# Compressing keys and values side by side in one pass of the weights

## The chip, the cores and the metric

The kernel runs on one NeuronCore of a Trainium2 chip. The metric is the device time of one execution in microseconds (us). The core has a matrix engine (TensorE, "PE", with its weight loads shown as "PEld"), a vector engine (VectorE, "DVE"), a scalar engine (ScalarE, "ACT"), a general engine (GpSimd, "POOL") and SyncE ("SP"), whose queue issues most of the transfers from memory.

## The reference

One transformer block on 512 tokens of width 2048 in float32, batch 1. What matters here:

```python
proj = h @ w_in                                  # then split: conv parts, q, kc, vc, ksl, vsl, kw, vw, gates
# kc, vc: the raw keys and values to be compressed, 512 tokens x 2 heads x 128

def compress(kv, pe, w1, b1, w2):
    n_cmp = (S - 32) // 16 + 1                   # 31 blocks of 32 tokens, one every 16
    idx = np.arange(n_cmp)[:, None] * 16 + np.arange(32)[None, :]
    blocks = kv[:, idx] + pe[None, None, :, None, :]
    hid = gelu(einsum('bnlgd,ldh->bngh', blocks, w1) + b1)   # w1: 32 x 128 x 256
    return einsum('bngh,he->bnge', hid, w2)

k_cmp = compress(k_cmp_raw, pe_k, k_w1, k_b1, k_w2)
v_cmp = compress(v_cmp_raw, pe_v, v_w1, v_b1, v_w2)
k_cmp = apply_rope(rms_norm(k_cmp, k_norm[0]), ...)
# then: attention of q over k_cmp/v_cmp, over selected and over windowed keys; output projection; gated FFN
```

So keys and values go through the same form of product: for each of 32 positions `l`, a 128 x 62 matrix (2 heads x 31 blocks) is multiplied with a 128 x 256 weight slice, and the 32 products are summed.

## The kernel before

The kernel is one long program written out by Python loops and ordered at build time by a planner, which goes by what is written first and by what its own model holds to be ready; on each engine, and on SP's queue, the instructions then run in that fixed order. Large products are done in three passes of a split float32 (`mm3`, lines 98 to 100: `hi x lo`, `lo x hi`, `hi x hi`); `load_split` (lines 83 to 94) takes a 512 KB piece of weights into a tile `raw`, rounds it on ACT (line 92, `whi`) and forms the rest on DVE (line 93, `wlo`).

The stage of interest stands between the start of the kernel (the adaptive norm and the first columns of `w_in`) and the convolution with attention. Two generators are woven together (line 528): `token_blocks` (line 521) does the projections of windowed keys/values and of the second half of the queries, each as 8 steps of `token_block`. A step loads one 512 KB piece (line 91), splits it, and runs 24 matmuls of 128 x 128 by 128 x 512 into four `main` banks of PSUM. At the end of each block of 8 steps the banks are read: `take_kv` (lines 427 to 434) and `take_q` (lines 420 to 425) norm and rotate (`normed_rope`: squares on ACT line 405, the root on ACT line 407, products with the rope tables on DVE lines 412 to 417), turn on TensorE (lines 432, 424) and copy. The next user of `main` waits for these reads.

`before_attention` (line 512) is the other generator: for every step of `token_blocks` it gets 1.5 turns. It first takes the four parts of `ksv` (`take_kv(0, ...)`) and the four of `q0` (`take_q(0, ...)`), two 8 KB-per-partition tiles filled by the stage before, and then goes through `compress`. There, for keys and then for values (loop over `m`, line 457), DVE adds the position term to the raw keys or values (`blocks`, line 467); then in 8 turns of 4 positions each, 512 KB of weights come into a tile of the same ring of four `raw` buffers that `load_split` uses (line 473) and are used as they are, in plain float32, by four matmuls (line 476):

```python
for ll in range(4):
    nc.tensor.matmul(ph[:NP_, 0:256], blocks[:, l + ll, :, :].rearrange("p g n -> p (g n)"), rv[:, ll, :], ...)
```

`NP_` is 62. The profile shows each of these matmuls as two records, so 64 matmuls are 128 records. After each loop the bias is added (line 481), gelu is taken on ACT (line 482) and the result is turned (line 485, copies line 486). The end of `compress` (lines 487 to 509) forms the compressed keys `kcT` and values `v4`. `compress` has 17 turns.

After the weave, `convs` and `attention_steps` are woven: a step of `conv` (line 679 is its load, 680 and 681 its split) takes three `main` banks, the second of them first. In the convolution stage `ada_steps` also loads pieces of `ada_w` (line 179) and sums them on DVE (line 189).

A ring tile is free for the next load when its last reader has run: a `load_split` tile after DVE's line 93, a compress tile after its four matmuls.

## Time and profile before

| | us |
|---|---|
| median of three runs | 2312.16 (2307.25 to 2317.63) |
| the profiled execution, its time | 2311.1 |
| the profiled execution, its span of instructions | 2309.3 |
| TensorE busy in it | 2234.3 (97%) |
| VectorE busy in it | 1681.4 (73%) |
| ScalarE busy in it | 960.3 (42%) |

The busy time of TensorE is the union of its records, whose ends are modelled and overlap: what a matmul costs in a stream is read from the distance between starts, not from its duration. The time outside the span is 2311.1 - 2309.3 = 1.8 us.

### The profile page before, as it was taken

The page shows a single profiled execution, that of the slowest core. Times are in us where ns is not written, and L with a number is a line of the kernel's source. Part 1 is how long each engine was busy: PE and PEld are TensorE (multiplying, and loading weights), DVE is VectorE, ACT ScalarE, POOL GpSimd, SP SyncE. Part 2 cuts the span into 40 slices and gives each one's busy share as a digit, 9 for nine tenths or more (in the row PEclk, how much of TensorE's full clock was granted, in tenths as well). Part 3 has the DMA queues.
Part 4 walks back from the last instruction along what each step waited for, and adds up shares of the span by engine and source line. Part 5 has one row for each costly group of instructions (what it writes and reads, how often), then busy time and mean ns, then how long its engine had stood idle before and what let it go on. Part 6 is the DMA issues. An engine that isn't in the chain of part 4 may idle for free.

```text
span 2309.3 us, 30022 instructions
## 1 busy us (share of the span) xinstructions
PE 2234.3 (97%) x11225; PEld 1861.8 (81%) x11225; DVE 1681.4 (73%) x2561; ACT 960.3 (42%) x1601; POOL 132.7 (6%) x204
## 2 busy tenths in 40 slices
PE   5889999999999999899999999999999999999999
PEld 4667767778777778788888888888888788888887
DVE  6897738877856783888888888888888655534356
ACT  6544425455444222744444444444444432222221
POOL 2430000000000000000000000000000200000010
PEclk9999999999999999999999999999999999999999
DMA  8884356544533883264334443344442675533243
GB/s 292 262 277 148 98 189 184 165 126 147 147 94 128 301 291 128 87 183 123 119 120 124 123 123 120 119 123 124 123 124 78 216 245 187 182 106 128 92 155 114
DMA packets 374406, 358.60 MB, mean 155 GB/s; under 512 B 14856, under 2 KB 288620, under 8 KB 373236
## 3 DMA queue, kind: packets, MB, share of 16 engines
q1 hardware_dynamic: 365364, 325.22, 44.7%
q0 software_dynamic: 8896, 31.46, 3.9%
q8 instruction: 88, 1.44, 0.2%
q14 instruction: 58, 0.48, 0.1%
HBM read 336.70 MB, written 19.92 MB: 154 GB/s over the span
## 4 chain that ended last, share of the span: by engine, by line
PE 42%; issue 36%; DVE 10%; DMA 9%; ACT 2%; POOL 1%; SPq 0%; DVEq 0%; POOLq 0%; ACTq 0%
PE main L98 8%; PE main L99 8%; PE main L100 8%; DMA araw<-in_ada_w 7%; DVE acc L189 4%; PE aux L98 4%; PE aux L99 4%; PE aux L100 4%; PE aux L646 1%; DVE wlo L93 1%; PE main L834 1%; PE aux L834 1%; PE aux L618 1%; POOL gd L886 1%; DMA raw<-in_w_in 1%
## 5 line engine op out<-in xcount | busy, mean ns | idle before, releaser
L92 ACT CAST whi<-raw 128x1024 fp32r<-128x1024 f32 (+1 forms) x168 | 171.7, 1022 | 486.9 <-PE main L100 265.9
L93 DVE TENSOR_TENSOR wlo<-raw,whi 128x1024 fp32r<-128x1024 f32 (+1 forms) x168 | 200.4, 1193 | 223.2 <-ACT whi L92 221.7
L834 PE MATMUL main<-hC,whi 128*128 128x512 f32 x1408 | 356.2, 395 | 5.5 <-DVE hC L851 3.3
L827 DVE TENSOR_TENSOR wlo<-raw,whi 128x1024 fp32r<-128x1024 f32 x218 | 265.8, 1220 | 107.1 <-ACT whi L822 107.1
L189 DVE SCALAR_TENSOR_TENSOR acc<-araw,cT,acc 128x512 f32<-128x512 f32 (+1 forms) x392 | 270.8, 692 | 90.1 <-DMA araw<-in_ada_w 79.3
L822 ACT CAST whi<-raw 128x1024 fp32r<-128x1024 f32 x218 | 228.1, 1046 | 259.5 <-PE main L834 129.4
L834 PEld LDWEIGHTS main<-hC,whi 128*128 128x128 f32 x1408 | 254.4, 190 | 52.2 <-DVE hC L851 4.4
L834 PE MATMUL aux<-hC,whi 128*128 128x512 f32 x1072 | 269.5, 393 | 0.0
L834 PEld LDWEIGHTS aux<-hC,whi 128*128 128x128 f32 x1072 | 193.6, 190 | 34.8
L836 PEld LDWEIGHTS main<-hC,wlo 128*128 128x128 f32 x1408 | 192.9, 191 | 13.8
L836 PE MATMUL main<-hC,wlo 128*128 128x256 f32 x1408 | 197.0, 283 | 0.0
L98 PE MATMUL main<-alo,whi 128*128 128x512 f32 x448 | 180.9, 404 | 9.9 <-DVE alo L296 9.9
L100 PE MATMUL main<-ahi,whi 128*128 128x512 f32 x448 | 177.2, 396 | 0.0
L99 PE MATMUL main<-ahi,wlo 128*128 128x512 f32 x448 | 177.0, 395 | 0.0
L836 PEld LDWEIGHTS aux<-hC,wlo 128*128 128x128 f32 x1072 | 146.4, 190 | 10.5
L98 PE MATMUL main<-wlo,ahi 128*128 128x512 f32 x384 | 152.3, 397 | 0.5 <-DVE t L773 0.4
L100 PE MATMUL main<-whi,ahi 128*128 128x512 f32 x384 | 150.6, 392 | 0.0
L99 PE MATMUL main<-whi,alo 128*128 128x512 f32 x384 | 150.6, 392 | 0.0
L836 PE MATMUL aux<-hC,wlo 128*128 128x256 f32 x1072 | 149.8, 282 | 0.0
L822 ACT CAST whi<-t 128x1024 fp32r<-128x1024 f32 x84 | 88.2, 1050 | 136.4 <-PE aux L834 70.9
L98 PE MATMUL main<-wlo,ghi 128*128 128x512 f32 x352 | 138.2, 394 | 3.0 <-ACT ghi L1056 2.7
L98 PE MATMUL aux<-wlo,ghi 128*128 128x512 f32 x352 | 137.8, 391 | 0.0
(273 smaller groups left out, 3818.8 us busy)
## 6 DMA issues: line engine op xcount, KB each, us to landing
raw<-in_ffn_w SPq DMA_DIRECT2D x264, 512.0 KB
araw<-in_ada_w SPq DMA_DIRECT2D x136, 512.0 KB
araw<-in_ada_w SPq DMA_DIRECT2D x112, 256.0 KB
raw<-in_w_in SPq DMA_DIRECT2D x128, 192.0 KB
raw<-in_w_in SPq DMA_DIRECT2D x40, 512.0 KB
raw<-in_w_out SPq DMA_DIRECT2D x32, 512.0 KB
gd<-d POOLq DMA_DIRECT2D x44, 256.0 KB, 2.3
graw<-gd POOLq DMA_DIRECT2D x44, 256.0 KB, 4.1
```

The costliest lines, as they stand in the source:

```text
L92: nc.scalar.copy(hi[:, :m], raw[:, :m])
L93: nc.vector.tensor_sub(lo[:, :m], raw[:, :m], hi[:, :m].bitcast(F32))
L98: nc.tensor.matmul(ps, lhs[0], rhs[1], start=first, stop=False)
L99: nc.tensor.matmul(ps, lhs[1], rhs[0], start=False, stop=False)
L100: nc.tensor.matmul(ps, lhs[0], rhs[0], start=False, stop=last)
L189: nc.vector.scalar_tensor_tensor(acc, w, s, acc, op0=ALU.mult, op1=ALU.add)
L618: nc.tensor.matmul(one[b], queries(g, i, h), kT[b][g][:, :L], start=True, stop=True)
L646: nc.tensor.matmul(po[:, b * HD:(b + 1) * HD], s["pT"][b][:, kb * P:(kb + 1) * P], vv[b][:, kb, g * HD:(g + 1) * HD], start=kb == 0, stop= ...
L822: nc.scalar.copy(hi, t)
L827: nc.vector.tensor_sub(lo, t, hi.bitcast(F32))
L834: nc.tensor.matmul(ps, wt[0][:, ks[k]], hC[p][:, k, :], start=first and k == 0, stop=False, skip_group_check=True)
L836: nc.tensor.matmul(ps[:, HS:], wt[1][:, ks[k]], hC[p][:, k, 0:HS], start=False, stop=last and k == HK - 1, skip_group_check=True)
```

## The change

Both loops of `compress` become one. The tile `ph` now holds keys in partitions 0 to 61 and values in partitions 64 to 125. For each position one matmul for keys and one for values follow each other, into these two groups of columns of the array. `blocks` is made for 8 positions at a time, for keys and values (16 additions of half the former size, two buffers each), ahead of every second turn. The weights of the keys keep coming through the ring of `raw` tiles, and the load of the next turn is written ahead of the matmuls of this one. The weights of the values come into four places of 512 KB that are the halves of `ksv` and `q0`: the first four loads stand at the head of `compress`, each later one behind the matmuls that used its place. The bias is added for each half, and gelu, and the two turns of `hid`, are done once for both; `hid` is set to zero first by POOL. `compress` now has 9 turns.

```diff
--- before.py
+++ after.py
@@ -454,36 +454,66 @@
         nc.sync.dma_start(per[:, 0, :], a["cmp_pe_k"][0])
         nc.sync.dma_start(per[:, 1, :], a["cmp_pe_v"][0])
         hidT = cpool.tile([P, 2, 2, NP_], F32, name="hidT")
-        for m, (w1n, b1n) in enumerate((("cmp_k_w1", "cmp_k_b1"), ("cmp_v_w1", "cmp_v_b1"))):
+        peT = cpool.tile([P, 2, CMP_BLOCK], F32, name="peT")
+        for m in range(2):
             pt = aux()
             nc.tensor.transpose(pt[:, :CMP_BLOCK], per[:, m, :], ident[:CMP_BLOCK, :CMP_BLOCK])
-            peT = cpool.tile([P, CMP_BLOCK], F32, tag="peT", name="peT")
-            nc.vector.tensor_copy(peT, pt[:, :CMP_BLOCK])
-            blocks = cpool.tile([P, CMP_BLOCK, NKV, NC_], F32, tag="blocks", name="blocks")
+            nc.vector.tensor_copy(peT[:, m, :], pt[:, :CMP_BLOCK])
+
+        def blocks(m, l):
+
+            t = cpool.tile([P, 8, NKV, NC_], F32, tag=f"blocks{m}", name=f"blocks{m}", bufs=2)
+            h = l // 16 * 16
             for g in range(NKV):
-                for h in range(2):
-
-                    src = raw_kv[:, m, g, h * 16:h * 16 + NC_ * 16].rearrange("p (n r) -> p r n", r=16)
-                    nc.vector.tensor_add(blocks[:, h * 16:(h + 1) * 16, g, :], src,
-                                         peT[:, h * 16:(h + 1) * 16, None].to_broadcast([P, 16, NC_]))
-            ph = aux()
-            for l in range(0, CMP_BLOCK, 4):
-                raw = ring[0].tile([P, 1024], F32, tag="raw", name="raw")
-                rv = raw.rearrange("p (l h) -> p l h", l=4)
-                nc.sync.dma_start(rv, a[w1n][0, l:l + 4].rearrange("l d h -> d l h"))
-                yield
-                for ll in range(4):
-                    nc.tensor.matmul(ph[:NP_, 0:256], blocks[:, l + ll, :, :].rearrange("p g n -> p (g n)"), rv[:, ll, :],
-                                     start=l + ll == 0, stop=l + ll == CMP_BLOCK - 1)
-            b1 = cpool.tile([NP_, 256], F32, tag="b1", name="b1")
-            nc.sync.dma_start(b1, a[b1n].to_broadcast([NP_, 256]))
-            hid = cpool.tile([NP_, 256], F32, tag="hid", name="hid")
-            nc.vector.tensor_add(hid, ph[:NP_, 0:256], b1)
-            nc.scalar.activation(hid, hid, AF.Gelu_apprx_tanh)
-            for h in range(2):
-                pt = aux()
-                nc.tensor.transpose(pt[:, :NP_], hid[:, h * P:(h + 1) * P], ident[:NP_, :NP_])
-                nc.vector.tensor_copy(hidT[:, m, h, :], pt[:, :NP_])
+                src = raw_kv[:, m, g, h:h + NC_ * 16].rearrange("p (n r) -> p r n", r=16)[:, l - h:l - h + 8, :]
+                nc.vector.tensor_add(t[:, :, g, :], src, peT[:, m, l:l + 8, None].to_broadcast([P, 8, NC_]))
+            return t
+
+
+        ph = aux()
+        at_m = (slice(0, NP_), slice(64, 64 + NP_))
+
+        places = [t[:, i:i + 2, :].rearrange("p a (b h) -> p (a b) h", b=2) for t in (ksv, q0) for i in (0, 2)]
+
+        def load_k(l):
+            raw = ring[0].tile([P, 1024], F32, tag="raw", name="raw")
+            rv = raw.rearrange("p (l h) -> p l h", l=4)
+            nc.sync.dma_start(rv, a["cmp_k_w1"][0, l:l + 4].rearrange("l d h -> d l h"))
+            return rv
+
+        def load_v(l):
+            rv = places[l // 4 % 4]
+            nc.sync.dma_start(rv, a["cmp_v_w1"][0, l:l + 4].rearrange("l d h -> d l h"))
+            return rv
+
+        vs = [load_v(l) for l in range(0, 16, 4)]
+        ks = load_k(0)
+        for l in range(0, CMP_BLOCK, 4):
+            if l % 8 == 0:
+                bl = [blocks(m, l) for m in range(2)]
+            yield
+            rvs = (ks, vs[l // 4])
+            if l + 4 < CMP_BLOCK:
+                ks = load_k(l + 4)
+            for ll in range(4):
+                for m in range(2):
+                    nc.tensor.matmul(ph[at_m[m], 0:256], bl[m][:, l % 8 + ll, :, :].rearrange("p g n -> p (g n)"),
+                                     rvs[m][:, ll, :], start=l + ll == 0, stop=l + ll == CMP_BLOCK - 1,
+                                     skip_group_check=True)
+            if l + 16 < CMP_BLOCK:
+                vs.append(load_v(l + 16))
+        b1 = cpool.tile([P, 256], F32, name="b1")
+        hid = cpool.tile([P, 256], F32, name="hid")
+        nc.gpsimd.memset(hid, 0.0)
+        for m, b1n in enumerate(("cmp_k_b1", "cmp_v_b1")):
+            nc.sync.dma_start(b1[at_m[m], :], a[b1n].to_broadcast([NP_, 256]))
+            nc.vector.tensor_add(hid[at_m[m], :], ph[at_m[m], 0:256], b1[at_m[m], :])
+        nc.scalar.activation(hid, hid, AF.Gelu_apprx_tanh)
+        for h in range(2):
+            pt = aux()
+            nc.tensor.transpose(pt[:, :P], hid[:, h * P:(h + 1) * P], ident)
+            for m in range(2):
+                nc.vector.tensor_copy(hidT[:, m, h, :], pt[:, at_m[m]])
         cw2 = cpool.tile([P, 2, 2, HD], F32, name="cw2")
         nc.sync.dma_start(cw2[:, 0], a["cmp_k_w2"][0].rearrange("(h p) e -> p h e", p=P))
         nc.sync.dma_start(cw2[:, 1], a["cmp_v_w2"][0].rearrange("(h p) e -> p h e", p=P))
```

## Rows read from the trace of the kernel before

**Rows 1.** The page's first part: busy time of each engine, its share of the span, instructions.

```profile
PE 2234.3 (97%) x11225; PEld 1861.8 (81%) x11225; DVE 1681.4 (73%) x2561; ACT 960.3 (42%) x1601; POOL 132.7 (6%) x204
```

**Rows 2.** Busy time by stretch. Columns: stretch, its length, busy time of each engine (instructions), granted clock of TensorE as a share of full speed, busy share of the DMA engines, GB/s moved. The first two rows cover the two token blocks, the third the end of the second, the fourth the convolution and attention behind it.

```profile
core 0: us, PE busy (x) PEld busy (x) DVE busy (x) ACT busy (x) POOL busy (x), PEclk, DMA share, GB/s
...
219.00:270.00 51.00, 50.05 (x229) 39.18 (x229) 43.53 (x114) 25.59 (x77) 0.32 (x1) 1.00 0.30 92
270.00:341.00 71.00, 69.56 (x300) 48.49 (x299) 25.55 (x46) 14.46 (x27) 0.00 (x0) 1.00 0.56 180
341.00:350.00 9.00, 8.03 (x39) 4.72 (x38) 8.23 (x19) 7.25 (x30) 0.00 (x0) 1.00 0.71 199
350.00:600.00 250.00, 245.79 (x1256) 198.08 (x1255) 197.52 (x436) 125.22 (x283) 0.00 (x0) 1.00 0.53 157
```

**Rows 3.** Groups of instructions between 240 and 365 us, shapes kept apart. Columns: line, engine, operation, tiles, shapes, count | busy us, mean ns of one | idle time before them and what ended it.

```profile
L476 PE MATMUL aux<-raw,blocks 128*62 128x256 f32 x128 | 30.4, 384 | 1.3 <-ACT rq L407 0.7 <-DVE blocks L467 0.5
...
L476 PEld LDWEIGHTS aux<-raw,blocks 128*62 128x62 f32 x128 | 16.2, 135 | 13.8 <-issue 2.5 <-ACT rq L407 1.1 <-DVE blocks L467 0.9
...
L467 DVE TENSOR_TENSOR blocks<-raw_kv,peT 128x496 f32<-128x496 f32 x8 | 7.6, 1027 | 0.1
...
L415 DVE TENSOR_TENSOR rw<-q,Zq 128x256 f32<-128x256 f32 x8 | 3.0, 419 | 0.0
```

**Rows 4.** TensorE's instructions in order of time, around two bursts of line 476 inside the second token block. Columns: start, length, what; in brackets idle time before it and what ended it.

```profile
305.64 0.39 PE L100 MATMUL main<-whi,ahi 128*128 128x512 f32 x1
305.96 1.94 PE L476 MATMUL aux<-raw,blocks 128*62 128x256 f32 x8
307.83 0.50 PE L98 MATMUL main<-wlo,ahi 128*128 128x512 f32 x1
308.16 0.39 PE L99 MATMUL main<-whi,alo 128*128 128x512 f32 x1
308.39 0.39 PE L100 MATMUL main<-whi,ahi 128*128 128x512 f32 x1
...
324.36 3.67 PE L476 MATMUL aux<-raw,blocks 128*62 128x256 f32 x16
```

**Rows 5.** TensorE in order of time: the first of the 24 matmuls of steps 9, 10 and 11 of the token blocks.

```profile
274.12 0.48 PE L98 MATMUL main<-wlo,ahi 128*128 128x512 f32 x1
...
283.44 0.50 PE L98 MATMUL main<-wlo,ahi 128*128 128x512 f32 x1
...
292.75 0.50 PE L98 MATMUL main<-wlo,ahi 128*128 128x512 f32 x1
```

**Rows 6.** SP's queue in order of time (start, time spent on issuing and waiting, what): loads of the token steps are line 91, of the compression line 473.

```profile
247.04 8.65 SPq L473 DMA_DIRECT2D raw<-in_cmp_k_w  x2
266.82 0.37 SPq L91 DMA_DIRECT2D raw<-in_w_in  x1
...
273.81 7.83 SPq L473 DMA_DIRECT2D raw<-in_cmp_k_w  x2
283.55 0.37 SPq L91 DMA_DIRECT2D raw<-in_w_in  x1
```

**Rows 7.** The chain that ended last, in order of time (start, length, what): the load of token step 10 and its split.

```profile
273.08 5.84 DMA raw<-in_w_in
278.94 1.05 ACT whi L92
280.02 1.23 DVE wlo L93
```

**Rows 8.** VectorE in order of time: the last reads of `q0`, and the split of token step 9.

```profile
258.55 0.75 DVE L415 TENSOR_TENSOR rw<-q,Zq 128x256 f32<-128x256 f32 x2
...
271.83 1.23 DVE L93 TENSOR_TENSOR wlo<-raw,whi 128x1024 fp32r<-128x1024 f32 x1 [1.40 <-ACT whi L92]
```

**Rows 9.** ScalarE in order of time: the first half of the split of token step 11.

```profile
287.55 1.05 ACT L92 CAST whi<-raw 128x1024 fp32r<-128x1024 f32 x1 [7.55 <-DMA raw<-in_w_in]
```

**Rows 10.** TensorE in order of time at the end of the second token block: the last matmul of its step 16, and all that runs until the convolution (line 98 with `alo`) has begun.

```profile
340.85 0.39 PE L100 MATMUL main<-whi,ahi 128*128 128x512 f32 x1
341.16 3.67 PE L476 MATMUL aux<-raw,blocks 128*62 128x256 f32 x16
345.14 0.66 PE L424 MATMUL aux<-const,ru 128*128 128x128 f32 x4 [0.31 <-DVE ru L417]
345.72 1.94 PE L476 MATMUL aux<-raw,blocks 128*62 128x256 f32 x8
347.59 0.50 PE L98 MATMUL main<-alo,whi 128*128 128x512 f32 x1
```

**Rows 11.** VectorE in the same stretch: reads of the first and of the second `main` bank (lines 412 and 415), and what stands between.

```profile
339.81 0.75 DVE L189 SCALAR_TENSOR_TENSOR acc<-araw,cT,acc 128x512 f32<-128x512 f32 x1 [3.05 <-DMA araw<-in_ada_w]
340.48 0.68 DVE L412 TENSOR_TENSOR ru<-main,Cq 128x512 f32<-128x512 f32 x1
341.08 0.75 DVE L415 TENSOR_TENSOR rw<-main,Zq 128x256 f32<-128x256 f32 x2
...
345.08 0.66 DVE L412 TENSOR_TENSOR ru<-main,Cq 128x512 f32<-128x512 f32 x1
345.66 0.75 DVE L415 TENSOR_TENSOR rw<-main,Zq 128x256 f32<-128x256 f32 x2
```

**Rows 12.** Waits of TensorE between 235 and 385 us: who waited for whom, us in total, times, longest.

```profile
PE aux L424 <- DVE ru L417: 1.5, 3, 0.7
```

## The prediction

> **What bounds the kernel now.** I read the busy times first: TensorE is busy 97% of the span, the next engine 73% [rows 1]. A share is an average, so the second view is the stretches around the change [rows 2]. From 219 to 341 us, where the two token blocks and the compression run, TensorE is busy 119.6 of 122 us; VectorE is busy 25.55 of 71 us in the second part, ScalarE 14.46, and transfers take 0.56 of the DMA engines. [...] Time taken off TensorE in this stage should therefore move everything behind it, as long as nothing the removed matmuls covered comes to light. The third view says what the compression costs TensorE: 128 records of line 476, 62 columns of the array wide [rows 3]. In order of time [rows 4] a burst of 16 records lasts 3.67 us and one of 8 lasts 1.94, so one record costs (3.67 - 1.94) / 8 = 0.216 us; the 0.384 of the group is a modelled, overlapping length. All 128 cost 27.7 us.

> **Pairing.** A key matmul and a value matmul now go to different columns of the array. No row of before shows two matmuls that write different columns of the array side by side, so the price lies between two ends. At one end they don't overlap, and the 27.7 us stay. At the other, two records run at a time: 64 x 0.216 = 13.8 us, a gain of 13.8. Each matmul is two records, in the order key, key, value, value; if a record waits only for the one ahead in its own columns, the second key record runs beside the first value record, the second value record beside the next key record, and only the first and last of a burst of 16 stand alone: 9 places instead of 16. Eight such bursts are 8 x 9 x 0.216 = 15.6 us, a gain of 12.1. I take this one, since the columns 62 to 127 are idle in every record of line 476 and the two products share neither weights, data nor output partitions.

> [...]

> **Edges of bursts.** Where line 476 begins and ends, the starts are 0.32 and 0.33 us apart, against 0.23 between two matmuls of line 99 and 100 [rows 4]: 0.19 us a burst. Sixteen groups of 8 records become eight of 16, some of both merged with a neighbour: at most 8 x 0.19 = 1.5, I take 1.0. TensorE's wait of 0.5 us for the additions of the values [rows 3] goes too, as these now come in quarters. Gross: 12.1 + 1.0 + 0.5 = 13.6 us. The two turns of `hid` that are saved are worth at most 0.3 (half of the 0.66 us of a burst of four turns [rows 10]); I take nothing.

> **Work beside TensorE.** Eight additions of 128 x 496 at 1.027 us become sixteen of 128 x 248. The nearest size, 128 x 256, takes 0.419 [rows 3]: 6.7 us in all against 8.2, and at the very worst 16 x 1.027 = 16.4. VectorE idles 45 of 71 us there, which hides either; without that cover the worst case would cost 8.2. One gelu less, one bias addition as before for each half, and a clearing of `hid` on POOL, which is busy 0.00 in that stretch [rows 2] and depends on nothing: taken at nothing, hidden by TensorE's 69.56 us.

> **Transfers.** Sixteen loads of 512 KB stay sixteen. The first four value loads wait for the last readers of `ksv` and `q0`, of which the last ends at 258.55 + 0.75 = 259.3 [rows 8]. Queued behind them on SP is the load of token step 9, and through it ScalarE's rounding, VectorE's rest and TensorE; but that load was held until 266.82 anyway [rows 6], so the wait is hidden by 7.5 us. The later four value loads become ready at the end of a burst, just when the loads of token steps do (283.55 stands right behind a burst). So their price is that of a neighbour in the queue: the load of step 10, between two compress loads, took 5.84 us [rows 6, 7], that of step 11, alone, from 283.55 to 287.55, 4.0 [rows 6, 9]: 1.8 us for a neighbour. What TensorE can bear: step 9's split ends at 273.06 [rows 8] and its matmuls start at 274.12 [rows 5], 1.1 us; step 10: 281.25 [rows 7] to 283.44, 2.2; step 11: 287.55 + 1.05 + 1.23 = 289.83 [rows 7, 9] to 292.75, 2.9. One more neighbour each costs 0.7 at step 9 and nothing after; two cost (3.6 - 1.1) + (3.6 - 2.2) + (3.6 - 2.9) = 4.6, and with a fourth step like the third 5.3. I take 1.0, bounds 0 and 5.3. In the steps with compression a turn has 16 records, but if they pair it lasts 1.94 us as now, so these distances hold.

> **The end of the stage.** `compress` now has 9 turns, not 17; at 1.5 turns a step it is done at step 12 of 16. Before, three groups of it stood between the last matmul of step 16, which ends its stream at about 341.1, and the first of the convolution, 347.59: 3.67 + 1.94 us [rows 10]. They covered the reading of the second `main` bank, which the convolution needs first, and which VectorE ends at 345.66 + 0.75 = 346.4 [rows 11]. That cover is gone. If VectorE's order stays, TensorE stands idle 346.4 - 341.1 - 0.66 (a burst of turns) = 4.6 us; if it gets there without the 3.05 us that it waited for a piece of `ada_w` [rows 11], 1.6. The waits that this place already had, 1.5 us [rows 12], are inside that. Loss: 0.1 to 3.1, I take 1.5. What follows in `compress` (gelu, turns, compressed keys) moves from under the convolution to under steps 13 to 16, both bound by TensorE.

> **Sum.** 13.6 - 1.0 - 1.5 = 11.1 us off the profiled execution's 2311.1 (span 2309.3 and 1.8 around it): **2300.0**. That execution lies 1.1 below the median of the runs, so the two agree. With the ends of the terms: best 13.8 + 1.5 + 0.5 - 0.1 = 15.7, so 2295.4; worst 12.1 + 0.5 - 5.3 - 3.1 = 4.2, so 2306.9.

> **Rivals.**
> No overlap: the array runs one record after the other whatever the columns. Then 1.0 + 0.5 is gained and 1.5 lost at the end of the stage, and bursts of 3.67 us leave transfers more room: 2311, 2309 to 2313. For it: no row shows an overlap, and every record of line 476 here takes its full 0.216. Against: nothing is shared. This is also how the change would not do what it says. 0.20.

> SP's queue turns into the bound, the one that ends on the other side: a value load ahead of a token load waits for the burst directly before that token step. Then a whole load and split are bare: 4.0 to 5.84 + 1.05 + 1.23 [rows 7, 9], 7.2 us on the mean. Two such steps (14.4) take the gain; four, steps 10 to 13, give 2300 + 28.8 = 2329. For it: SP does stand still for 8.65 and 7.83 us at loads of line 473 [rows 6]. Against: the token loads wait for the same bursts already, and a planner that finds a token load ready first issues it first. 0.10.

> Weight loads bare: the pairs don't overlap and neither do loads of one half with matmuls of the other: 128 x 0.135 us [rows 3] = 17.3, so 2311 + 17 = 2328. [...] 0.06.

> **Chances and range.** The forecast holds 0.64. Half a per cent is 11.6 us, about what the measurement can tell from no change (the three runs lie 10.4 apart), and my gain of 11.1 stands on that edge: faster by more 0.40, within 0.24, as the term of the pairs may reach 13.8 and the start of the convolution may be free. No overlap: within 0.19, slower 0.01. SP's queue: slower 0.08, within 0.02. Bare loads: slower 0.05, within 0.01. Together faster 0.40, within 0.46, slower 0.14. The range goes from 2295 (0.05 below) to 2316, which takes in no overlap and leaves out 0.13; the likeliest case alone spans 2295 to 2307.

> **What would show it.** In the profile after, pairing is right if a burst of 16 records takes about 2.1 us rather than 3.67, with starts of key and value records nearly together; wrong if starts are 0.216 apart. The edge term shows as fewer bursts. The transfer term shows as idle time of TensorE before line 98 at steps 9 to 13, put down to `wlo`. The last term shows as idle time between the last matmul of step 16 and the convolution; more than 5 us there, or work of attention drawn forward to fill it, would put me wrong by some us either way, as would a planner that orders the convolution stage otherwise.

## The result, and the profile after

The changed kernel took 2293.88 us (median of four runs, 2292.26 to 2294.74) against 2313.31 for the kernel before (four runs, 2307.25 to 2317.63): a ratio of 0.9917, with an interval from 0.9893 to 0.9941. The forecast was 2300.0 with a range from 2295; the gain is about 19 us where 11.1 were worked out. The direction held, and so did the pairing; two losses that were charged against it did not come, and the time lies 1.1 us outside the range. (The same program, measured again in runs 5 and 8 below, gained 15 and 17 us.) The profiled execution took 2294.12 us, its span is 2292.4.

In the changed kernel line 476 (the matmuls of the compression) has become line 500, 467 (additions) 469, 473 (loads) 481 for keys and 486 for values, 482 (gelu) 511, 485 (turns of `hid`) 514, and 681 (split of the convolution's weights) 711. The first row is the page's busy time of each engine; [rows 1] answers to it.

```profile
PE 2220.5 (97%) x11223; PEld 1856.7 (81%) x11223; DVE 1684.2 (73%) x2569; ACT 958.6 (42%) x1598; POOL 132.0 (6%) x205
```

TensorE's busy time fell by 13.8 us, and its share stayed. By stretch (the columns of [rows 2]), the stage of the compression and what follows it:

```profile
219.00:270.00 51.00, 50.79 (x238) 39.53 (x238) 43.58 (x118) 25.39 (x75) 0.80 (x2) 1.00 0.47 144
270.00:341.00 71.00, 70.01 (x369) 52.14 (x368) 42.91 (x97) 23.89 (x64) 0.00 (x0) 1.00 0.61 188
...
350.00:600.00 250.00, 247.63 (x1257) 199.06 (x1256) 198.62 (x424) 126.68 (x291) 0.52 (x1) 1.00 0.53 152
```

Against [rows 2] TensorE is fuller in every stretch: it did not only lose work, it also lost idle time, 0.74, 0.45 and 1.84 us in these three. VectorE took over work of the convolution stage earlier (42.91 us busy where it was 25.55), and hid it.

TensorE in order of time, as in [rows 4]: first the first burst of line 500, then two turns that follow each other directly. `raw` is the weight of the keys, `ksv` or `q` that of the values.

```profile
263.24 0.61 PE L500 MATMUL aux<-raw,blocks 128*62 128x256 f32 x2
263.79 0.50 PE L100 MATMUL main<-whi,ahi 128*128 128x512 f32 x1
264.22 0.43 PE L500 MATMUL aux<-ksv,blocks 128*62 128x256 f32 x1
264.23 0.43 PE L500 MATMUL aux<-raw,blocks 128*62 128x256 f32 x1
264.49 0.38 PE L500 MATMUL aux<-ksv,blocks 128*62 128x256 f32 x1
264.49 0.38 PE L500 MATMUL aux<-raw,blocks 128*62 128x256 f32 x1
...
270.41 0.43 PE L500 MATMUL aux<-raw,blocks 128*62 128x256 f32 x1
270.42 0.43 PE L500 MATMUL aux<-ksv,blocks 128*62 128x256 f32 x1
270.68 0.38 PE L500 MATMUL aux<-raw,blocks 128*62 128x256 f32 x1
270.68 0.38 PE L500 MATMUL aux<-ksv,blocks 128*62 128x256 f32 x1
...
273.70 0.38 PE L500 MATMUL aux<-raw,blocks 128*62 128x256 f32 x1
273.70 0.38 PE L500 MATMUL aux<-q,blocks 128*62 128x256 f32 x1
274.01 0.66 PE L432 MATMUL aux<-const,ru 128*128 128x128 f32 x4
```

From 270.41 the 32 records of two turns start in pairs, the two of a pair at most 0.01 us apart, and the pairs follow each other about every 0.216 us: 274.01 - 270.41 = 3.60 us for 32 records, about the length of 16 before [rows 4]. So there are 8 places (of 0.216 us each) in a turn here, not the 9 of the forecast. Four matmuls, eight records, run without a partner: one key and one value matmul at the ends of the first turn, and one of each around 282.36 and 291.62, where the planner put the first key matmul of a turn ahead of a token step. In all the 128 records take 68 places.

The first burst says why. There the first key matmul (both records, 263.24) runs alone, a matmul of line 100 follows, and at 264.22 the first value record starts, when the additions of the values are done (its weight load, below, waits 0.25 us for line 469). A key record starts 0.01 us behind it. In program order the second record of that value matmul stands ahead of this key record, and yet the two start together: each half of the columns takes its own records in its own order here, and the key record of 264.23 does not wait for the value record of 264.49. Experiment 4 below shows how far that reaches.

The weight load of that first value record, and those of a pair (the view of TensorE's loads in order of time):

```profile
264.22 0.13 PEld L500 LDWEIGHTS aux<-ksv,blocks 128*62 128x62 f32 x1 [0.25 <-DVE blocks L469]
...
270.68 0.14 PEld L500 LDWEIGHTS aux<-raw,blocks 128*62 128x62 f32 x1
270.69 0.14 PEld L500 LDWEIGHTS aux<-ksv,blocks 128*62 128x62 f32 x1
```

Two loads of 0.14 us fall in a place of 0.216 and cost nothing to be seen.

TensorE's waits from 219 to 400 us (what it waited for, us in total, times, longest):

```profile
PE aux L732 <- ACT cc L730: 0.8, 1, 0.8
PE aux L514 <- ACT hid L511: 0.6, 1, 0.6
PE aux L667 <- DVE gsc L208: 0.4, 1, 0.4
PE aux L424 <- DVE ru L417: 0.4, 1, 0.4
PE aux L432 <- DVE ru L417: 0.2, 1, 0.2
```

In the same view of the kernel before, line 432 stood with

```profile
PE aux L432 <- DVE ru L417: 1.1, 2, 0.9
```

In the list of after no wait is for `wlo` and none for a weight. The 1.3 us of line 476 [rows 3] are gone, of the 1.5 us of line 424 [rows 12] 0.4 are left, and of the 1.1 of line 432 0.2; the wait for gelu (0.6) is new.

The end of the stage, TensorE in order of time and then VectorE's split of the convolution's first weights (line 711) and its reading of the `main` banks:

```profile
332.18 0.39 PE L100 MATMUL main<-whi,ahi 128*128 128x512 f32 x1
332.41 0.41 PE L98 MATMUL main<-alo,whi 128*128 128x512 f32 x1
```

```profile
322.99 0.95 DVE L711 TENSOR_TENSOR wlo<-raw,whi 128x768 fp32r<-128x768 f32 x1
...
331.48 0.73 DVE L415 TENSOR_TENSOR rw<-main,Zq 128x256 f32<-128x256 f32 x2
...
334.64 0.75 DVE L415 TENSOR_TENSOR rw<-main,Zq 128x256 f32<-128x256 f32 x2
```

The convolution's first matmul (332.41) stands 0.23 us behind the last one of step 16, the distance between two matmuls of lines 99 and 100 in [rows 4]. The bank that became free last before it is the one read until 331.48 + 0.73 = 332.2; the next was read until 334.64 + 0.75 = 335.4, long behind that start. The 1.6 to 4.6 us of idle time that the prediction saw here don't exist.

**Where the 20 us went.** I took the time from the start of each TensorE instruction to the next, less the idle time, grouped by line, and also the distance between the same matmul in both profiles. From the same matmul at about 219 us to the one at 590.36 before and 570.24 after:

| | before | after | difference |
|---|---|---|---|
| matmuls of the compression, start to next start | 29.6 | 15.7 | -13.9 |
| TensorE idle | 7.5 | 3.5 | -4.0 |
| the rest (turns, edges of bursts) | | | -2.4 |
| total | | | -20.3 |

From there to the end some 3 us are given back in this pair of profiles (the spans differ by 16.9), 2.4 of them between 770 and 860 us, where the granted clock is 0.93 and 0.91 in two stretches of after and 1.00 in those of before. No instruction of the change stands there; run 8 shows how much two executions of one kernel can differ in that way. The table is of one pair of executions too: in run 8's profile the idle time of this stretch is 4.9 us, not 3.5.

### The profile page after: what moved, and what is told of

The parts are those of the page before. It is cut to its first block, busy times and chain, and to the rows that moved or that the text cites. A ratio compares the mean times of both kernels' runs of the same rounds, so it can differ in the third digit from the quotient of the medians.

```text
span 2292.4 us, 30011 instructions
## 1 busy us (share of the span) xinstructions
PE 2220.5 (97%) x11223; PEld 1856.7 (81%) x11223; DVE 1684.2 (73%) x2569; ACT 958.6 (42%) x1598; POOL 132.0 (6%) x205
## 4 chain that ended last, share of the span: by engine, by line
PE 45%; issue 36%; DVE 9%; DMA 7%; ACT 2%; POOL 1%; SPq 0%; POOLq 0%; DVEq 0%; ACTq 0%
PE main L98 8%; PE main L100 8%; PE main L99 8%; DMA araw<-in_ada_w 5%; DVE acc L189 4%; PE aux L98 4%; PE aux L100 4%; PE aux L99 4%; PE aux L676 2%; PE aux L648 1%; DVE wlo L93 1%; DMA raw<-in_w_in 1%; POOL gd L916 1%; PE aux L864 1%; PE main L864 1%
## 5 line engine op out<-in xcount | busy, mean ns | idle before, releaser
L852 ACT CAST whi<-raw 128x1024 fp32r<-128x1024 f32 x218 | 228.2, 1047 | 259.3 <-PE main L864 129.1
L866 PEld LDWEIGHTS main<-hC,wlo 128*128 128x128 f32 x1408 | 192.9, 191 | 13.9
```

What stands on the lines that cost most here:

```text
L852: nc.scalar.copy(hi, t)
L866: nc.tensor.matmul(ps[:, HS:], wt[1][:, ks[k]], hC[p][:, k, 0:HS], start=False, stop=last and k == HK - 1, skip_group_check=True)
```

## The experiments

**What was to be told apart.** The first theory is the prediction's with the corrected count: the overlap of the column halves gives 64 x 0.216 = 13.8 us, and the rest is edges and waits. Its rivals: the gain, or what is above the 11.1, comes from the compression being over earlier; from the places, that is, from the weights no longer competing for ring tiles; or from the loads being asked for a step ahead. The first four kernels ran beside 23 runs of the kernel before (median 2315.56 us), the other four beside 17 (2314.82). None of them leaves out work. The expectations were written before the runs and say what each theory gives.

**1. No overlap: both products in the same columns.** Each product gets a bank of its own, and the bias is read accordingly; everything else is as in the changed kernel.

```diff
-        ph = aux()
+        ph = [aux(), aux()]
-                    nc.tensor.matmul(ph[at_m[m], 0:256], ...
+                    nc.tensor.matmul(ph[m][:NP_, 0:256], ...
...
```

> Keys and values in turn as in the changed kernel, with its loads, places and turns, but both products written to partitions 0 to 61, each in its own bank of PSUM, so that both use the same columns of the array. Theory A (the overlap of the two groups of columns is the gain): 128 records one after the other again, 64 x 0.216 = 13.8 us more than the changed kernel, about 2308 us (2305 to 2311), still some 5 below the kernel before. Theory B (most of the gain comes from loads, turns and an earlier end of the compression): within 4 us of the changed kernel, 2292 to 2298.

Measured: 2313.51 us (2309.98 to 2317.07), ratio 0.9985 (0.9977 to 0.9994), above both expected ranges and nearer to the first. TensorE in order of time, inside a burst of two turns:

```profile
273.02 0.59 PE L500 MATMUL aux<-ksv,blocks 128*62 128x256 f32 x2
273.45 0.59 PE L500 MATMUL aux<-raw,blocks 128*62 128x256 f32 x2
```

Two records per 0.43 us, one after the other: the matmuls of line 500 take 28.7 us. With the overlap undone, the change is worth 2.1 us by the medians (1.4 to 5.3 by the interval). Against run 3, on the same chip and with the same number of matmuls, the overlap is worth 2313.51 - 2295.94 = 17.6 us; against runs 5 and 8, which are the changed kernel on another chip, 13.7 and 15.8. 13.0 of it is line 500 itself (28.7 - 15.7). The rest is not put to single lines (TensorE waits 1.2 us for gelu here instead of 0.6), and it is no more than executions of one kernel differ by.

**2. Pairing alone: both weights through the ring, asked for ahead of their own turn.** The columns as in the change; no places (`load_v` takes a ring tile as `load_k` does), no lead.

```diff
-        vs = [load_v(l) for l in range(0, 16, 4)]
-        ks = load_k(0)
         for l in range(0, CMP_BLOCK, 4):
+            rvs = (load_k(l), load_v(l))
             yield
-            rvs = (ks, vs[l // 4])
...
```

> The pairing alone: both weights come through the ring of four raw tiles, loaded ahead of their own turn as in the kernel before; ksv and q0 are not used as places. Theory A: the overlap is what counts and loads are hidden, 2292 to 2297 us. Theory C (the places and the lead carry part of the gain, since a turn now needs two of four ring tiles and a token load waits for a burst): waits of TensorE for wlo of 2 to 6 us at each of the token steps 9 to 12, 2300 to 2315 us.

Measured: 2311.0 us (2306.41 to 2318.59), ratio 0.9979 (0.9969 to 0.9989), a gain of some 5 us, as the expectation's theory C has it, though most of the waits are for other weights than it names. TensorE's waits from 219 to 400 us, and one of them in order of time:

```profile
PE aux L497 <- DMA raw<-in_cmp_k_w: 7.5, 3, 3.5
...
PE main L98 <- DVE wlo L93: 1.3, 3, 0.6
```

```profile
306.12 0.99 PE L497 MATMUL aux<-raw,blocks 128*62 128x256 f32 x2 [3.51 <-DMA raw<-in_cmp_k_w]
```

The pairs overlap here too, but TensorE, which is now done with a turn in half the time, stands still until the next weights come: 7.5 us for key weights, and 1.3 for splits of the token blocks, of which the same view of before lists none. Behind the two longest of these waits, 3.14 and 3.51 us, the granted clock is 0.83 from 270 to 280 us and 0.57 from 306 to 310 (0.97 over all from 219 to 345, where the kernel before has 1.00), which adds to the loss. So most of the gain of the overlap reaches the end only because of where the weights go. (This run drops the lead along with the places; a lead without places was not run.)

**3. The compression stretched: two `yield` a turn, 17 turns as before.**

```diff
             yield
+            yield
```

> The changed kernel with two yields a turn, so that the compression has 17 turns again and ends with the second token block, as before. If my term for the end of the stage were right (bursts cover the reading of the main banks, and 1.5 us are lost without them), this is 1 to 3 us faster than the changed kernel: 2291 to 2293. If the early end is itself part of what the change gained beyond the overlap, it is 3 to 5 us slower: 2297 to 2299. If neither, the same within 2 us.

Measured: 2295.94 us (2294.34 to 2297.75), ratio 0.9914 (0.9901 to 0.9927): no slower than the changed kernel (0.9917, and 0.9925 and 0.9929 in runs 8 and 5), and not faster by more than its executions differ. That the compression's matmuls are over at 307 us instead of at the end of the stage (333.9 here) is not where the gain comes from. This takes away the rival of the early end. For the prediction's term of 1.5 us at the end of the stage these times alone would be too coarse; there the rows above decide.

**4. Four key matmuls, then four value matmuls.**

```diff
-            for ll in range(4):
-                for m in range(2):
+            for m in range(2):
+                for ll in range(4):
```

> The changed kernel with the four key matmuls of a turn first and its four value matmuls behind them, instead of in turn. If records start strictly in the order of the program, only the last key record and the first value record of a turn run together and nearly the whole 13.8 us come back: 2306 to 2309. If each group of columns takes its own records as soon as they are queued, whatever stands between, nothing is lost: 2292 to 2296.

Measured: 2300.78 us (2298.14 to 2307.91), ratio 0.9941 (0.9926 to 0.9956), between the two expected ranges. In the first turn the value records also wait for their additions, which end at about 266.1, so the burst to read is the second, of two turns. TensorE in order of time:

```profile
272.63 1.29 PE L500 MATMUL aux<-raw,blocks 128*62 128x256 f32 x5
273.55 0.43 PE L500 MATMUL aux<-ksv,blocks 128*62 128x256 f32 x1
273.76 0.38 PE L500 MATMUL aux<-raw,blocks 128*62 128x256 f32 x1
...
277.26 0.66 PE L432 MATMUL aux<-const,ru 128*128 128x128 f32 x4
```

Eight key records stand ahead of the first value record. That starts at 273.55, about when the fifth key record does: four key records go by alone at the start of the burst, four value records alone at its end, and what lies between is paired. The burst takes 277.26 - 272.63 = 4.63 us where the same 32 records take 3.60 in the changed kernel. Line 500 takes 20.0 us in all instead of 15.7; these 4.3 are most of the 4.8 between this run and run 3. So TensorE reached past waiting records of the other half here, but only past some four of them.

**5. Key weights not asked for a step ahead.** Places kept.

```diff
-        ks = load_k(0)
         for l in range(0, CMP_BLOCK, 4):
+            ks = load_k(l)
...
-            if l + 4 < CMP_BLOCK:
-                ks = load_k(l + 4)
```

> The changed kernel with the key weights loaded ahead of their own turn, as in the kernel before, instead of a step ahead; the places for the values stay. Theory C in the form that the places alone carry the gain of the loads: the same as the changed kernel, 2293 to 2298 us, and no wait of TensorE for raw tiles between 260 and 320 us. If the lead of the keys is needed: waits for key weights as in the run with both in the ring, 2300 to 2311.

Measured: 2299.77 us (2295.16 to 2302.93), ratio 0.9929 (0.9917 to 0.9942), between the two expected ranges and, beside run 8 (0.9925), the same as the changed kernel. But this run does not test the lead: the planner put all loads of SP's queue, and all instructions of every engine, into the order that they have in the changed kernel, over the whole trace. What was written differently came out the same, so this is one more measurement of the changed kernel (with a wait of 0.8 us for one split that the first profile does not have). What the lead is worth stays open.

**6. Two by two: two key matmuls, two value matmuls, and so on.**

```diff
-            for ll in range(4):
-                for m in range(2):
+            for ll, m in ((0, 0), (1, 0), (0, 1), (1, 1), (2, 0), (3, 0), (2, 1), (3, 1)):
```

> The changed kernel with two key matmuls, then two value matmuls, in turn. With four by four the first value record started beside the fifth key record, so TensorE reaches about four records past the one it runs. If that reach is the cause of the loss there, two by two (four records of each) loses next to nothing: within 2 us of the changed kernel, bursts of 16 records of 1.9 to 2.2 us. If every change from one group of columns to the other costs something, the loss lies between: 3 us.

Measured: 2295.66 us (2293.67 to 2298.09), ratio 0.9916 (0.9903 to 0.9928): nothing lost. The first key records, which run alone, and the start of the second burst:

```profile
263.84 1.05 PE L500 MATMUL aux<-raw,blocks 128*62 128x256 f32 x4
...
271.15 0.43 PE L500 MATMUL aux<-raw,blocks 128*62 128x256 f32 x1
271.17 0.43 PE L500 MATMUL aux<-ksv,blocks 128*62 128x256 f32 x1
```

The first four key records run alone because the values' additions are not done (the first value weight load, at 264.75, waits 0.32 us for line 469). In the second burst the first value record starts 0.02 us behind the first key record, although three more key records stand ahead of it. With four records between the halves TensorE still pairs, with eight it does not quite: the reach of about four records from run 4 holds.

**7. Places alone: the kernel before, with its value weights in the places of `ksv` and `q0`.** No pairing, no lead.

```diff
+            places = [t[:, i:i + 2, :].rearrange("p a (b h) -> p (a b) h", b=2) for t in (ksv, q0) for i in (0, 2)]
...
-                raw = ring[0].tile([P, 1024], F32, tag="raw", name="raw")
-                rv = raw.rearrange("p (l h) -> p l h", l=4)
+                if m:
+                    rv = places[l // 4 % 4]
+                else:
+                    raw = ring[0].tile([P, 1024], F32, tag="raw", name="raw")
+                    rv = raw.rearrange("p (l h) -> p l h", l=4)
```

> The kernel before, keys and then values in the same columns, with one part of the change alone: the value weights come to the places of ksv and q0 and no longer through the ring. Theory D (TensorE sets the time, the loads were hidden already): the same as before within 2 us, 2312 to 2317. Theory E (the ring was already holding the stage up, and what the change gained beyond the overlap comes from the places): 3 to 5 us faster, 2309 to 2312.

Measured: 2313.37 us (2308.8 to 2316.67), ratio 0.9987 (0.9978 to 0.9996): a gain of 1.5 us by the medians, 3 by the ratio (0.9 to 5.1 by the interval), inside theory D's range. Before the pairing nearly every load was hidden, so places had little to give. Pairing alone (run 2) gives 5 us and places alone 1.5 to 3, both together 15 to 19 (the result and runs 5 and 8): some 7 to 12 us are there only when both are done.

**8. The changed kernel once more, unaltered**, to see what two executions of it differ by.

> The changed kernel again, unchanged, beside the others: ratio to the kernel before 0.990 to 0.993. Its profile tells which of the differences in the stages behind the convolution (the granted clock at the turns of x2, and the waits of attention) are of the kernel and which of one execution.

Measured: 2297.7 us (2292.61 to 2303.3), ratio 0.9925 (0.991 to 0.994). Its profile (span 2300.3) is 8 us longer than the first profile of this kernel, with the same instructions in the same order. Of these 2.0 are there by 122 us, 2.8 between 307 and 332, 2.8 between 755 and 798. The last is two waits that are longer (for a piece of `ada_w` summed by VectorE, 3.6 us against 2.6, and 1.7, which the first profile lacks, for VectorE's scaling of the output projection's banks). The middle one can be followed to its start. First the chain that ended last and VectorE, ScalarE, TensorE in order of time; then the stretch from 316 to 320:

```profile
302.89 6.72 DMA raw<-in_w_in
```

```profile
310.80 1.23 DVE L93 TENSOR_TENSOR wlo<-raw,whi 128x1024 fp32r<-128x1024 f32 x1 [2.80 <-ACT whi L92]
311.94 0.85 DVE L510 TENSOR_TENSOR hid<-aux,b 62x256 f32<-62x256 f32 x2
...
312.87 1.28 ACT L511 ACT_TABLE_LOAD   x1 [2.10 <-DVE hid L510]
...
314.63 0.44 PE L514 MATMUL aux<-const,hid 128*128 128x128 f32 x2 [1.85 <-ACT hid L511]
...
316.50 0.63 PE L100 MATMUL main<-whi,ahi 128*128 128x512 f32 x1
316.93 0.63 PE L98 MATMUL main<-wlo,ahi 128*128 128x512 f32 x1
```

```profile
316.00:320.00 4.00, 4.00 (x12) 3.12 (x11) 2.16 (x8) 2.22 (x5) 0.00 (x0) 0.57 0.41 115
```

The load of a token step took 6.72 us here and 5.83 in the first profile, behind one of 6.43 us that took 5.86 in the first. TensorE bears that (its matmuls of that step come later), but on VectorE the bias additions of the compression (line 510, 311.94) stand behind the split (310.80), gelu and its table behind them, and the turns of `hid` on TensorE behind that. The wait of 0.6 us becomes 1.85. Then the granted clock is 0.57 from 316 to 320 us: matmuls start 0.43 us apart instead of 0.23, until 319.49. In the first profile the granted clock stayed at 1.00 in the same place after its wait of 0.63. Eight matmuls at 0.20 more are 1.6 us, more than the 1.2 by which the wait grew.

## Why the prediction was wrong in size and right in kind

**The bound** held: TensorE was and is the bound of the stage (from 219 to 341 us busy 119.6 of 122 us before and 120.8 after), and what came off it came off the end.

**Pairing, the largest term: 12.1 forecast, 13.0 measured.** The step "only the first and last of a burst of 16 stand alone: 9 places instead of 16" was wrong: 8 x 9 = 72 places were forecast, 68 were found, 60 of 0.216 us less than the 128 before. It supposed that the records start in program order; under the condition that it names, that a record waits only for the one ahead in its own columns, the count would have been 8. The rows show just that, two streams in which each half takes its own records; the four places above 64 are the matmuls without a partner, which the prediction did not have.

**Edges and waits of the values: 1.0 + 0.5 forecast.** The size was nearly right. Start to next start, line 476 took 29.6 us for 27.7 of work in 13 bursts, and line 500 15.7 for 14.7 (68 places) in 7: 0.9 less on the line itself. Another 0.09 (0.32 - 0.23) ahead of each of the six bursts that are gone, 0.5, is part of the 2.4 of the rest, of which 1.9 are not taken apart. The wait of 0.5 for the additions went, and with it the 0.7 for `rq` [rows 3], which I had not counted.

**Transfers: 1.0 of loss forecast, 0 in the first profile.** This is one of the two losses that did not come. The neighbours in the queue cost what was said: the load of one token step took 5.56 us, and the chain that ended last runs over it:

```profile
283.81 5.56 DMA raw<-in_w_in
289.40 1.06 ACT whi L92
290.48 1.24 DVE wlo L93
```

The split is done at 291.72 and the step's matmuls start at 292.14, behind a burst of two turns, so 0.4 us of the forecast's 2.9 were left, and at the step before 0.05 (split done at 282.83, matmuls at 282.88). The slack was used up almost exactly, and was enough; run 2 shows what happens when it isn't, run 5 has one wait of 0.8 us for a split, and run 8 shows that a late load can still come out by way of VectorE's order.

**The end of the stage: 1.5 of loss forecast, none found, and old waits gone.** This is the step that failed outright: "the second `main` bank, which the convolution needs first". The convolution started with the bank that was free, 0.23 us behind the matmul ahead of it, and 3 us before the second bank was read. [rows 11] could have told it: the first bank was read by 341.08 + 0.75 = 341.8, with the convolution at 347.59 [rows 10]. The bursts of line 476 stood ahead of the convolution in program order. What the first of them did cover is another wait, which the prediction did not look at, that for the split of the convolution's own first weights; VectorE in the kernel before:

```profile
343.52 0.95 DVE L681 TENSOR_TENSOR wlo<-raw,whi 128x768 fp32r<-128x768 f32 x1
```

That split ended at 344.5; after, the loads for it are issued from 305 us on instead of from 336, and it is done at 322.99 + 0.95 = 323.9, so nothing was left to cover. The waits that this stage already had, which I had left inside the loss, went down as well: lines 424 and 432 lose 1.2 and 0.9 us, and a wait of 1.0 us for a turn of attention at 586 us (line 664) has no counterpart after, which may be chance of the execution.

**Work beside TensorE** was hidden as said. The additions took longer than the 0.419 that I took from the nearest row: 16 in a median of 0.572 us, 9.2 in all instead of 6.7, still without effect, with one wait of 0.2 us of the loads on them.

**The sum.** Forecast 11.1; up to 590 us 20.3 were measured in the profiles. The difference of 9.2 is 0.9 (pairing) + 6.0 (idle time: 4.0 gained where 0.5 gained and 2.5 lost were forecast) + 2.3 (edges and the rest, 0.9 + 2.4 against 1.0). So the larger part of the miss is two losses that did not come and waits that went away, not the overlap. The range's lower end took the best ends of all terms and had only 0.5 for waits that vanish; that is why it was too narrow. That the time fell outside by 1.1 us is partly chance: the same program took 2297.7 and 2299.77 us in runs 8 and 5, inside the range, though their gains of 17 and 15 us are above the 11.1 as well.

**The rivals.** No overlap was priced at no gain, and run 1, which makes it so, gave 2.1 us (2313.51 where before gave 2315.56): that price was right to about 2 us. SP's queue did not become the bound (from 219 to 400 us TensorE waits for no weight and no split), and bare weight loads did not appear: the pairs follow each other every 0.216 us with two loads of 0.14 in each, as the records of before did with one of 0.135 [rows 3]. What the prediction didn't have as a rival is what run 2 showed: without the places, the pairing would have starved itself.

## What to carry to other kernels

When two small products share no weights, data or output partitions, put them in different columns of the array and alternate them closely: here two products 62 columns wide took 15.7 us, where they had taken 29.6 one after the other. Halving the matrix time doubles the rate at which weights are wanted, so look for buffers that are free in that stage before counting the gain (5 us without, 15 to 19 with). And before a burst is called the cover of a wait, see in the rows which wait it is, and whether the work behind it needs what is waited for.

## What the runs showed of the hardware

A wait was dearer than its length in run 8: behind 1.85 us of idle TensorE the granted clock stood at 0.57 for the 4 us from 316 to 320, 1.6 us more for eight matmuls, and behind 0.63 us in the same place of the first profile at 1.00. But the length of the wait did not decide it alone. In the kernel before, a longer one was followed by nothing of the kind (TensorE in order of time, then the stretch around it):

```profile
798.33 0.63 PE L206 MATMUL aux<-const,acc 128*128 128x128 f32 x4 [2.72 <-DVE acc L189]
...
790.00:816.00 26.00, 23.28 (x112) 19.01 (x111) 17.44 (x23) 7.26 (x11) 1.10 (x2) 1.00 0.88 305
```

At the same place after, behind 2.55 us, it was 0.79 from 776 to 784 us. Where the clock falls differs from execution to execution of the same kernel: from 100 to 135 us it was 0.95 in the longer of its two profiles and 1.00 in the other, which I did not follow to a cause.
